# Encoder layer on one core: small vectors fetched during the first SwiGLU, halves of three Hyena columns among its norm, two gate columns beside the last convolution

## The chip, the cores and the metric

The kernel runs on 1 core of one Trainium2 chip. The metric is device microseconds of one execution; the time before is 2900.08 us, the median of 3 runs (2899.32 to 2900.85 us).

## The reference

One layer of a hybrid encoder on 1 x 1024 x 1024 float32:

```
x = x + 1/2 * SwiGLU_1(RMSNorm(x))
u_hy, u_rw, g_hy, g_rw = split(RMSNorm(x) @ w_in)        # 1536 | 1952 | 1024 | 1024 columns
y_hy = hyena(u_hy)   # width-3 conv, z = x1 * long_conv(v), z = x2 * long_conv(z), z @ hy_out
y_rw = rwkv7(u_rw)   # token shift, two directions of a 64x64-state scan, group norm, gate, rw_out
x = x + (sigmoid(g_hy) * y_hy + sigmoid(g_rw) * y_rw) @ w_out
x = x + 1/2 * SwiGLU_2(RMSNorm(x))
out = RMSNorm(x)
```

The Hyena filters come from a small sine network over positions and are normalised per channel. Each elementwise stage needs vectors of a few hundred to a few thousand numbers: convolution taps and bias (4 x 1536), token-shift mixes (2 x 1952), RWKV offsets and scales (5 x 512), norm weights and the like.

## The kernel before

**Matmuls.** Every large product is done three times over in split form (`mm3`): hi x hi, lo x hi and hi x lo, each 128 x 512. `w_hi` is cast by ScalarE, `w_lo` is a difference made by GpSimd or VectorE (`col_weights`). The length of 1024 is kept in two halves, t = 0 and t = 1 (`hl[0]`, `hl[1]`; in the order rows hThi_101/hTlo_102 before and hThi_111/hTlo_112 after are half 0, hThi_106/hTlo_107 before and hThi_119/hTlo_120 after half 1). A half of a 128-wide column of `w_in` is 24 matmuls.

**Order.** The kernel is written as Python generators. A scheduler puts the instructions of each engine into one fixed order from their program order, their dependences and its own durations; matmuls that go through `InOrder` keep program order among themselves. TensorE, VectorE, ScalarE and the DMA queue of SyncE (SP) each run their list in order. PSUM pools set which results can be in flight: `pgu` (4 banks) for gate/up, `pw` (3 banks) for columns of `w_in`.

**Stages by the trace.** Load of x with transposes (`load_xT`, to 41 us); first SwiGLU (`ffn`, 41 to 776); the mixer's norm (`Norm.rows`, `spread`, `apply`: VectorE makes nm_h, its hi and lo parts are the next stage's operand); `mixer_in`, which begins with the small vectors rw_kk, rw_head, rw_mu, hy_cw and hf_vec, then 12 Hyena columns (`column`, `hyena_short_conv`) with `hyena_hidden` and `hyena_filters` as background (795 to 1068); `rwkv_columns`, a dense stream of 16 columns beside the long convolutions (`long_convs`, 1069 to 1369); the RWKV scan (`Rwkv.run`) with the gate columns as its filling (`mixer_gates`: 16 columns x 2 halves, each yielding twice, so 64 pieces of 12 matmuls; then `hyena_out` and `RwkvPost`; 1369 to about 1985); the output products (to 2170); second SwiGLU and final norm.

**What feeds the scan.** `Rwkv.__init__` loads its constants, and `rates` and `prep` its first inputs (rl_x, rl_r, rl_k, rl_kh); on SP these stand among the last stores of the convolution stage. `Rwkv.run` yields at each step; at each yield one piece of filling is taken.

Of the kernel before, what the change touches and what calls it, by code (L numbers as in the profile page):

```python
# [13 lines left out]
F32 = mybir.dt.float32  # L14
# [6 lines left out]
P = 128  # L21
L = 1024
# [158 lines left out]
def ffn(nc, pools, wp, xT, hl, w_gu, w_down, done, half_done):  # L181

    def gu_weights(f):
        return [col_weights(nc, wp, w_gu[:, c * DFF + f * P : c * DFF + (f + 1) * P], KD) for c in (0, 1)]
# [3 lines left out]
    two, dn, pmm = pools()  # L190
# [3 lines left out]
    for gi, gn in enumerate(FF_GROUPS):  # L194
        gs = []
        for f in range(f0, f0 + gn):
# [5 lines left out]
            for t in range(2):  # L202
                pg, pu = [pmm.tile([P, 512], F32, name="pgu", tag="pgu", bufs=4) for _ in (0, 1)]
# [37 lines left out]
        f0 += gn  # L241

# [63 lines left out]
def hyena_hidden(tc, I, h2):  # L306

    nc = tc.nc
    with ExitStack() as ctx:
# [8 lines left out]
        vec = one.tile([64, 3], F32, name="hf_vec")  # L318
        for j, nm in enumerate(("hy_sin_freq", "hy_ffn_b1", "hy_ffn_b2")):
            nc.sync.dma_start(vec[:, j : j + 1], I[nm].unsqueeze(1))  # L320
        nc.vector.tensor_scalar(vec[:, 1:3], vec[:, 1:3], vec[:, 0:1], None, ALU.mult)
# [19 lines left out]
def hyena_filters(tc, ctx, I, h2, k_dram, scl):  # L341
# [9 lines left out]
    tneg = one.tile([P, RT], F32, name="tneg")  # L351
    nc.sync.dma_start(tneg, I["c_tneg"])
# [134 lines left out]
def hyena_vectors(nc, pool, I):  # L487

    cw = pool.tile([P, 12, 4], F32, name="hy_cw")
    for j in range(3):  # L490
        nc.sync.dma_start(cw[:, :, j], I["hy_conv_w"][j].rearrange("(t p) -> p t", p=P))
    nc.sync.dma_start(cw[:, :, 3], I["hy_conv_b"].rearrange("(t p) -> p t", p=P))
    return cw


def hyena_short_conv(nc, pool, xpool, psum, ident, ps, cw, dst):


    u = pool.tile([P, L + 2], F32, name="sh_u", tag="sh_u")
    nc.vector.memset(u[:, 0:1], 0.0)  # L500
    nc.vector.memset(u[:, L + 1 : L + 2], 0.0)
    uc = pool.tile([P, RT, P], F32, name="sh_o", tag="sh_o")
    ucv = uc.rearrange("p r m -> p m r")
    for t in range(2):
        nc.scalar.copy(u[:, 1 + 512 * t : 513 + 512 * t], ps[t])
        nc.scalar.activation(ucv[:, ts(t, 64), :], ps[t].rearrange("p (m r) -> p m r", r=RT),
                             AF.Identity, bias=cw[:, 3:4], scale=cw[:, 1:2])
    for j in (0, 2):
        nc.vector.scalar_tensor_tensor(ucv, u[:, j : j + L].rearrange("p (m r) -> p m r", r=RT),
                                       cw[:, j : j + 1], ucv, ALU.mult, ALU.add)  # L510
# [299 lines left out]
class Rwkv:  # L810
# [6 lines left out]
    def __init__(self, tc, ctx, I, dr, ident):  # L817
        self.tc, self.nc, self.I, self.dr, self.ident = tc, tc.nc, I, dr, ident
# [926 lines left out]
```

## Time and profile before

| | us |
|---|---|
| median of 3 runs | 2900.08 |
| profiled execution, its time | 2905.31 |
| its span | 2903.5 |
| TensorE busy | 2718.3 |
| VectorE busy | 1232.0 |
| ScalarE busy | 905.1 |
| GpSimd busy | 555.4 |
| mean granted TensorE clock | 0.966 |

Busy time is per engine and counts overlapping instructions once. A timeline row gives an instruction's start and length and, in brackets, the idle time of the engine just before it with what ended it. A window's row gives the busy time of each engine in that stretch with the number of instructions, the granted clock and the DMA engines' share. A line number is that of the kernel before.

### The profile page before, as it was taken

To read this page: it belongs to the slowest core of one execution; us is meant where nothing else is said; L and a number is where in the kernel's file an instruction comes from. 1 tells how busy PE (TensorE), PEld (TensorE's weight loads), DVE (VectorE), ACT (ScalarE), POOL (GpSimd) and SP (SyncE) were. 2 spreads that over 40 slices of the span, in tenths; PEclk is the share of its full clock that TensorE was granted. 3 is DMA by queue.
4 is the path that set the end of the run, shared out by engine and by line. 5 is a ranking of instruction groups with operands and counts; after the bars stand their busy time and mean duration, and the time that the engine had idled before them with its cause. 6 is when DMAs were issued, how large, how long until landed. Compare 5 with 4: busy or idle time off the path is not lost. (4 is left out here: it accounts for less than half of the span.)

```text
span 2903.5 us, 46061 instructions
## 1 busy us (share of the span) xinstructions
PE 2718.3 (94%) x19440; PEld 2198.2 (76%) x19440; DVE 1232.0 (42%) x2141; ACT 905.1 (31%) x1517; POOL 555.4 (19%) x351
## 2 busy tenths in 40 slices
PE   7999999999689899987899999797999999999998
PEld 6888888888566677775787787675778888888887
DVE  4111110111547669898765566756560111101014
ACT  4111111111445443333554555522332111111112
POOL 2323233232414210000000000000033232223322
PEclk9999999999899999998999999898999999999999
DMA  4111111111342245554445334457631111111102
GB/s 123 51 44 51 44 55 47 41 54 41 112 134 69 91 129 179 149 168 127 135 125 160 102 113 148 145 161 234 189 87 54 49 51 44 55 40 53 48 27 91
DMA packets 408990, 277.49 MB, mean 96 GB/s; under 512 B 51107, under 2 KB 369135, under 8 KB 408144
## 3 DMA queue, kind: packets, MB, share of 16 engines
q1 hardware_dynamic: 408784, 274.55, 31.7%
q8 instruction: 153, 2.51, 0.4%
q14 instruction: 53, 0.43, 0.0%
HBM read 203.58 MB, written 70.91 MB: 95 GB/s over the span
## 5 line engine op out<-in xcount | busy, mean ns | idle before, releaser
L43 PE MATMUL pgu<-hThi,w_hi 128*128 128x512 f32 x1408 | 554.1, 394 | 0.8 <-issue 0.8
L45 PE MATMUL pgu<-hThi,w_lo 128*128 128x512 f32 x1408 | 551.4, 392 | 0.0
L44 PE MATMUL pgu<-hTlo,w_hi 128*128 128x512 f32 x1408 | 548.4, 390 | 0.5 <-DVE hTlo L37 0.3
L210 DVE TENSOR_TENSOR silu<-silu,pgu 128x512 f32<-128x512 f32 x88 | 60.5, 688 | 892.2 <-PE pgu L45 882.7
L33 ACT CAST w_hi<-w_st 128x1024 fp32r<-128x1024 f32 (+1 forms) x180 | 175.5, 976 | 496.2 <-PE pgu L44 320.4
L37 POOL TENSOR_TENSOR w_lo<-w_st,w_hi 128x1024 fp32r<-128x1024 f32 x100 | 240.4, 2404 | 413.2 <-ACT w_hi L33 407.5
L45 PEld LDWEIGHTS pgu<-hThi,w_lo 128*128 128x128 f32 x1408 | 264.6, 188 | 60.5
L44 PEld LDWEIGHTS pgu<-hTlo,w_hi 128*128 128x128 f32 x1408 | 264.6, 188 | 59.1 <-DVE hTlo L37 0.7
L43 PEld LDWEIGHTS pgu<-hThi,w_hi 128*128 128x128 f32 x1408 | 264.7, 188 | 55.8 <-issue 1.2
L43 PE MATMUL pdn<-g_hi,wd_hi 128*128 128x512 f32 x704 | 274.9, 391 | 4.6 <-DVE xT L227 4.6
L44 PE MATMUL pdn<-g_lo,wd_hi 128*128 128x512 f32 x704 | 274.4, 390 | 2.0 <-POOL g_lo L37 2.0
L45 PE MATMUL pdn<-g_hi,wd_lo 128*128 128x512 f32 x704 | 274.8, 390 | 1.5 <-POOL wd_lo L37 1.5
L227 DVE SCALAR_TENSOR_TENSOR xT<-pdn,xT 128x512 f32<-128x512 f32 x192 | 132.4, 691 | 315.3 <-PE pdn L45 315.3
L43 PE MATMUL pw<-hThi,w_hi 128*128 128x512 f32 (+1 forms) x448 | 186.4, 416 | 18.5 <-DVE nm_h L123 10.0
L45 PE MATMUL pw<-hThi,w_lo 128*128 128x512 f32 (+1 forms) x448 | 186.8, 418 | 12.1 <-DVE w_lo L1228 12.1
L37 POOL TENSOR_TENSOR wd_lo<-wdst,wd_hi 128x512 fp32r<-128x512 f32 (+1 forms) x112 | 132.9, 1187 | 332.8 <-ACT wd_hi L33 332.8
L37 POOL TENSOR_TENSOR g_lo<-silu,g_hi 128x512 fp32r<-128x512 f32 x88 | 113.9, 1294 | 397.2 <-ACT g_hi L33 397.2
L44 PE MATMUL pw<-hTlo,w_hi 128*128 128x512 f32 (+1 forms) x448 | 184.6, 412 | 0.0
L33 ACT CAST wd_hi<-wdst 128x512 fp32r<-128x512 f32 (+1 forms) x112 | 64.4, 576 | 379.1 <-PE pdn L44 360.7
L37 POOL TENSOR_TENSOR hTlo<-nm_h,hThi 128x512 fp32r<-128x512 f32 x16 | 23.1, 1444 | 802.9 <-ACT hThi L33 802.9
L43 PEld LDWEIGHTS pdn<-g_hi,wd_hi 128*128 128x128 f32 x704 | 132.2, 188 | 33.2 <-ACT wd_hi L33 4.0
L44 PEld LDWEIGHTS pdn<-g_lo,wd_hi 128*128 128x128 f32 x704 | 132.2, 188 | 30.8 <-POOL g_lo L37 2.9
(312 smaller groups left out, 4245.5 us busy)
## 6 DMA issues: line engine op xcount, KB each, us to landing
w_st<-in_ffn_w_gu SPq DMA_DIRECT2D x88, 512.0 KB, 3.9
w_st<-in_w_in SPq DMA_DIRECT2D x59, 512.0 KB, 4.2
wdst<-in_ffn_w_down SPq DMA_DIRECT2D x64, 256.0 KB, 2.8
wdst<-in_ffn_w_down SPq DMA_DIRECT2D x48, 192.0 KB, 2.5
d_kf<-kout SPq DMA_DIRECT2D x32, 256.0 KB, 2.2
hy_k<-d_kf SPq DMA_DIRECT2D x32, 256.0 KB, 3.2
w_st<-in_w_out SPq DMA_DIRECT2D x16, 512.0 KB, 4.4
d_X<-sh_x SPq DMA_DIRECT2D x12, 512.0 KB, 3.5
```

Of the source, the lines that this page charges most:

```text
L33: nc.scalar.copy(hi, src)
L37: eng.tensor_tensor(lo, src, hi.bitcast(F32), ALU.subtract)
L43: te.matmul(out, lhs[0], rhs[0], start=first, stop=False)
L44: te.matmul(out, lhs[0], rhs[1], start=False, stop=False)
L45: te.matmul(out, lhs[1], rhs[0], start=False, stop=last)
L210: nc.vector.tensor_tensor(sl, sl, pu, ALU.mult)
L227: nc.vector.scalar_tensor_tensor(xa, ps, 0.5, xa, ALU.mult, ALU.add)
```

## The change

1. A class `Constants` keeps all small vectors in SBUF for the whole kernel. It holds a list of 34 small pieces of work (26 DMAs and 8 VectorE operations); the first SwiGLU's loop takes one at each of its yields. The loads at the old places go (in `Norm`, `hyena_hidden`, `hyena_filters`, `hyena_vectors`, `mixer_in`, `Rwkv`, `RwkvPost`).
2. The 3 `pw` banks are opened ahead of the first SwiGLU, whose gate and up products use them too; the load's transposes have 4 banks of their own.
3. `hyena_short_conv` becomes `ShortConv` with `take(t)` and `finish`; the t = 0 halves of the columns 8, 9 and 10 (72 matmuls) are written ahead of all else in `mixer_in`.
4. `N_GB = 2`: gate columns 0 and 1 (both halves, 96 matmuls) stand at the end of `rwkv_columns`; `mixer_gates` starts at column 2, so 56 pieces are left of 64.
5. `Rwkv.run` yields labels. Which steps get no piece, and which get `hyena_out` or `RwkvPost`, is chosen by label instead of by count; the first elimination has 6 yields instead of 4; `hyena_out` begins earlier; c_start, c_mask and c_eye are loaded after the first `rates`.

```diff
+class Constants:
+    def __init__(self, nc, pool, I):
+        load = lambda out, src: todo(lambda: nc.sync.dma_start(out, src))
+        cols = lambda ap: ap.rearrange("(t p) -> p t", p=P)
+        for j in range(3):
+            load(self.cw[:, :, j], cols(I["hy_conv_w"][j]))
+        load(self.cw[:, :, 3], cols(I["hy_conv_b"]))
...
+        for j in range(2):
+            load(mu[:, 0:15, j], cols(I["rw_mu"][j, 0:1920]))
+            load(mu[0:32, 15, j], I["rw_mu"][j, 1920:1952])
+        for m in (mu[:, 0:15], mu[0:32, 15:16]):
+            todo(lambda m=m: nc.vector.tensor_tensor(m[:, :, 2], m[:, :, 0], m[:, :, 1], ALU.add))
...
-                pg, pu = [pmm.tile([P, 512], F32, name="pgu", tag="pgu", bufs=4) for _ in (0, 1)]
+                pg, pu = [bank() for _ in (0, 1)]
...
-                with tc.tile_pool(name="ldx", bufs=1) as lp:
-                    load = load_xT(nc, lp, pmm, ident, g1, x, xT, hl, "pgu", 4)
+                with tc.tile_pool(name="ldx", bufs=1) as lp, tc.tile_pool(name="ldp", bufs=4, space=PSUM) as lps:
+                    load = load_xT(nc, lp, lps, ident, g1, x, xT, hl, "ld_ps", 4)
...
+                work = iter(K.work)
                 for _ in ff:
-                    pass
+                    next(work, lambda: None)()
...
+            w = {t: weights(t) for t in order[0:3]}
+            ps0 = {t: half(w[t], 0) for t in order[0:3]}
+            for t in order[0:2]:
+                convs[t] = conv(t)
+                convs[t].take(0, ps0.pop(t))
...
+                    else:
+                        nc.scalar.activation(o[:, ts(t, 512)], ps, AF.Tanh, scale=0.5)
+                        if t:
+                            nc.sync.dma_start(dr["sgh"][ts(j - 16, P)], o)
...
-            for j in range(16):
+            for j in range(N_GB, 16):
...
-        for _ in range(4):
-            yield
+        for _ in range(6):
+            yield (-1, "eliminate")
...
+        free = [(s, n) for s in range(-1, NB) for n in ("inverse3", "pv")] + [(3, "ws"), (4, "ws")]
         for _ in mixer_gates(tc, I, wp, h0, hctx, hB, dr):
-            next(rw)
-            n += 1
-            if n % 11 == 2 and 2 < n < 68:
-                next(rw)
-                n += 1
+            while (at := next(rw)) in free:
+                pass
```

VectorE in the load of x, ahead of the operands of half 1 (rms_e, rms_r: the norm's scale; ld_x: the scaled input). Before:

```order
L70 TENSOR_TENSOR rms_e<-rms_e,rms_t 128x4
L71 TENSOR_SCALAR rms_e<-rms_e 128x4
L72 TENSOR_TENSOR rms_r<-rms_r,rms_e 128x4
L148 TENSOR_SCALAR ld_x<-ld_x,rms_r 128x1024 x2
L155 SCALAR_TENSOR_TENSOR hTlo_107<-ld_ps,nm_g_125,hThi_106 128x512 x8
L210 TENSOR_TENSOR silu<-silu,pgu 128x512 x8
```

The same place after (k_kk, k_mu: small vectors):

```order
L265 TENSOR_SCALAR k_kk<-k_kk 128x4
L70 TENSOR_TENSOR rms_e<-rms_e,rms_t 128x4
L71 TENSOR_SCALAR rms_e<-rms_e 128x4
L72 TENSOR_TENSOR rms_r<-rms_r,rms_e 128x4
L146 TENSOR_SCALAR ld_x<-ld_x,rms_r 128x1024 x2
L273 TENSOR_TENSOR k_mu<-k_mu 128x15
L273 TENSOR_TENSOR k_mu<-k_mu 32x1
L274 TENSOR_SCALAR k_mu<-k_mu 128x15
L274 TENSOR_SCALAR k_mu<-k_mu 32x1
L153 SCALAR_TENSOR_TENSOR hTlo_120<-ld_ps,nm_g_135,hThi_119 128x512 x8
```

The operations on small vectors, each behind its DMA, now stand ahead of the lo parts of half 1. On TensorE, the 48 matmuls of the first gate/up pair on half 0 stand among the load's 128 transposes, where before all came behind them.

TensorE at the end of the first SwiGLU (pdn: its down product; nm_ps: the norm's sums and their spreading). Before:

```order
L44 MATMUL pdn<-g_lo,wd_hi 128x512
L45 MATMUL pdn<-g_hi,wd_lo 128x512
L106 MATMUL nm_ps<-ones_c,nm_acc 128x1 x4
L116 MATMUL nm_ps<-nm_d,ones_c 128x128 x4
L43 MATMUL pw<-hThi_101,w_hi 128x512
L44 MATMUL pw<-hTlo_102,w_hi 128x512
L45 MATMUL pw<-hThi_101,w_lo 128x512
```

After:

```order
L45 MATMUL pw<-hThi_111,w_lo 128x512
L104 MATMUL nm_ps<-ones_c,nm_acc 128x1 x4
L43 MATMUL pw<-hThi_111,w_hi 128x512
L44 MATMUL pw<-hTlo_112,w_hi 128x512
L45 MATMUL pw<-hThi_111,w_lo 128x512
L43 MATMUL pw<-hThi_111,w_hi 128x512
L44 MATMUL pw<-hTlo_112,w_hi 128x512
L45 MATMUL pw<-hThi_111,w_lo 128x512
L43 MATMUL pw<-hThi_111,w_hi 128x512
L44 MATMUL pw<-hTlo_112,w_hi 128x512
L114 MATMUL nm_ps<-nm_d,ones_c 128x128 x2
```

Matmuls of the columns 8 to 10 on half 0 stand between the norm's two steps for half 1; of the 72, 12 stand among the last down products, 24 around the norm's steps and 36 behind them.

TensorE at the end of the last convolution (hy_y: its inverse transform; hy_t: the turned result). Before:

```order
L618 MATMUL hy_y<-cxt,Dm 128x256 x8
L721 MATMUL hy_t<-ident,hy_z 128x128 x4
L618 MATMUL hy_y<-cxt,Dm 128x256 x4
L721 MATMUL hy_t<-ident,hy_z 128x128 x8
L618 MATMUL hy_y<-cxt,Dm 128x256 x4
L721 MATMUL hy_t<-ident,hy_z 128x128 x4
L55 MATMUL pw<-hThi_101,w_hi 128x512
```

A piece of the same place after:

```order
L764 MATMUL hy_t<-ident,hy_z 128x128 x4
L45 MATMUL pw<-hThi_111,w_lo 128x512
L43 MATMUL pw<-hThi_111,w_hi 128x512
L44 MATMUL pw<-hTlo_112,w_hi 128x512
L764 MATMUL hy_t<-ident,hy_z 128x128 x4
L661 MATMUL hy_y<-cxt,Dm 128x256 x4
L45 MATMUL pw<-hThi_111,w_lo 128x512
L43 MATMUL pw<-hThi_111,w_hi 128x512
L44 MATMUL pw<-hTlo_112,w_hi 128x512
L45 MATMUL pw<-hThi_111,w_lo 128x512
L764 MATMUL hy_t<-ident,hy_z 128x128 x4
```

Of the 96 matmuls of the gate columns, 74 stand ahead of the last hy_t (43 of them ahead of the first hy_y here) and 22 behind it; 12 of `mixer_gates` follow, then the scan's first product.

SP at the same place (d_z: the convolution's result; d_sgh: the gates; rw_w, rw_a, rw_start, rw_mask, rw_eye, rl_x: the scan's). Before, rl_x stood some rows ahead of the last hy_x load, and d_z behind that. After:

```order
L769 DMA d_z<-hy_zT 128x2x1024
L876 DMA rw_w_9123<-in_rw_w 128x512
L876 DMA rw_a_9124<-in_rw_a 128x512
L1274 DMA d_sgh<-sh_o 128x1024
L902 DMA rl_x<-d_tw 128x128
L903 DMA rl_x<-d_ad 128x128
L1162 DMA rw_start<-in_c_start 128x512
L1162 DMA rw_mask<-in_c_mask 128x128
L1162 DMA rw_eye<-in_c_eye 128x256
```

The scan's first loads now stand behind the store of the convolution's result and behind the store of the second gate column.

## Rows read from the trace of the kernel before

**Rows 1.** The page, part 1: busy time, share of the span, instructions.

```profile
PE 2718.3 (94%) x19440; PEld 2198.2 (76%) x19440; DVE 1232.0 (42%) x2141; ACT 905.1 (31%) x1517; POOL 555.4 (19%) x351
```

**Rows 2.** Windows: start:end, length, busy (instructions) of PE, PEld, DVE, ACT, POOL, PEclk, DMA.

```profile
100.00:150.00 50.00, 50.00 (x222) 41.20 (x221) 6.90 (x10) 9.45 (x13) 17.25 (x10) 1.00 0.20 58
...
860.00:1068.00 208.00, 189.96 (x765) 141.32 (x764) 147.78 (x268) 104.73 (x152) 57.97 (x34) 0.95 0.26 81
1069.00:1338.00 269.00, 247.91 (x1119) 199.59 (x1118) 234.38 (x354) 91.34 (x132) 0.00 (x0) 0.96 0.55 164
...
1369.00:1960.00 591.00, 543.41 (x9920) 447.13 (x9920) 382.78 (x783) 289.51 (x617) 0.00 (x0) 0.94 0.46 138
```

**Rows 3.** Timeline of PE in the load: start, length, line, what, [idle before].

```profile
25.51 5.20 PE L141 MATMUL ld_ps<-ident,ld_x 128*128 128x128 f32 x32
35.16 6.10 PE L152 MATMUL ld_ps<-ident,ld_x 128*128 128x128 f32 x32 [4.44 <-DVE ld_x L148]
41.26 0.50 PE L43 MATMUL pgu<-hThi,w_hi 128*128 128x512 f32 x1
```

**Rows 4.** Windows, as rows 2, of the norm and the first Hyena columns.

```profile
775.70:822.10 46.40, 28.22 (x104) 22.43 (x104) 19.71 (x42) 12.53 (x19) 9.08 (x6) 0.74 0.44 118
795.00:800.00 5.00, 4.47 (x11) 3.53 (x12) 1.19 (x7) 0.62 (x1) 1.27 (x1) 0.50 0.73 263
```

**Rows 5.** Timeline of PE: the first Hyena column and the Hyena network's first matmul.

```profile
795.53 0.76 PE L43 MATMUL pw<-hThi,w_hi 128*128 128x512 f32 x1 [10.01 <-DVE nm_h L123]
...
822.10 1.07 PE L331 MATMUL ps_h<-feats,w 33*64 33x512 f32 x2
```

**Rows 6.** Windows, as rows 2, of the last convolution's end.

```profile
1339.00:1369.40 30.40, 12.82 (x50) 9.75 (x49) 26.78 (x43) 8.89 (x14) 0.95 (x1) 0.78 0.48 131
```

**Rows 7.** Waits of PE from 1069 to 1369.4: us in total, times, longest.

```profile
PE pw L45 <- DVE w_lo L1228: 12.1, 3, 6.4
PE hy_y L618 <- DVE cxt L533: 10.9, 1, 10.9
```

**Rows 8.** Timeline of DVE in the load: the lo parts of half 1.

```profile
37.82 5.36 DVE L155 SCALAR_TENSOR_TENSOR hTlo<-ld_ps,nm_g,hThi 128x512 fp32r<-128x512 f32 x8 [2.15 <-ACT hThi L154]
```

**Rows 9.** Timeline of SP's DMA queue in the load.

```profile
31.76 1.59 SPq L215 DMA_DIRECT2D wdst<-in_ffn_w_down  x2
61.39 0.37 SPq L172 DMA_DIRECT2D w_st<-in_ffn_w_gu  x1
```

**Rows 10.** Timelines of SP, ACT and DVE where the small vectors are fetched.

```profile
808.83 3.20 SPq L491 DMA_DIRECT2D hy_cw<-in_hy_conv_w  x3
...
815.61 3.24 ACT L506 ACTIVATE sh_o<-pw,hy_cw 128x512 f32<-128x512 f32 x3 [0.68 <-DMA hy_cw<-in_hy_conv_b]
...
810.97 1.20 DVE L1199 TENSOR_TENSOR rw_mu<-rw_mu 128x15 f32<-128x15 f32 x1 [13.20 <-DMA rw_mu<-in_rw_mu]
```

**Rows 11.** One tile's operations on DVE: durations in ns, lowest/median/highest.

```profile
L1228 DVE TENSOR_TENSOR w_lo<-w_st,w_hi x16: 421/1218/1226, 1016.9 to 1308.6; 128x1024 fp32r<-128x1024 f32 x15, 128x256 fp32r<-128x256 f32 x1
```

**Rows 12.** Timeline of PE from the convolution's end to the first inverse.

```profile
1369.39 0.50 PE L55 MATMUL pw<-hThi,w_hi 128*128 128x512 f32 x1 [1.16 <-ACT hy_zT L723]
...
1373.93 1.16 PE L55 MATMUL psA<-rl_x,rw_w 64*128 64x128 f32 x16
...
1418.42 1.78 PE L55 MATMUL psA<-rw_xt,rw_a 32*32 32x16 f32 x118 [6.39 <-DVE rw_xt L984]
```

**Rows 13.** Timeline of SP's DMA queue at the convolution's end.

```profile
1347.78 0.50 SPq L868 DMA_DIRECT2D rl_x<-d_tw  x1
...
1369.36 0.37 SPq L726 DMA_DIRECT2D d_z<-hy_zT  x1
```

**Rows 14.** A window, as rows 2, of one scan step's middle.

```profile
1640.00:1650.00 10.00, 8.77 (x141) 7.06 (x141) 8.90 (x16) 10.00 (x27) 0.00 (x0) 1.00 0.45 150
```

**Rows 15.** Waits of PE from 1369 to 1960: us in total, times, longest.

```profile
PE psA L58 <- ACT rw_BT L955: 4.9, 4, 1.2
PE pz L55 <- ACT w_hi L33: 4.9, 1, 4.9
```

More of the change, by code (lines that the diff above doesn't have):

```diff
@@ L189, in ffn @@
     yield
-    two, dn, pmm = pools()
+    two, dn, pmm, bank = pools()
     wd_v = w_down.rearrange("(f p) d -> p f d", p=P)
@@ L317, in hyena_hidden @@
         nc.sync.dma_start(w2, I["hy_ffn_w2"])
[L318 to L321, printed above, removed]
+        vec = K.hidden
         feats = one.tile([33, L], F32, name="feats")
@@ L1114, in invert @@
             job = self.merge(x)
[L1115 to L1126 removed]
+            for i in range(4):
+                next(job, None)
+                if i < 2:
+                    self.transposes(x, i, "AV")
+                else:
+                    next(rates, None)
+                yield (x["s"] - 1, f"inverse{i}")
             return y
@@ L1131, in run @@
             pass
+        for t, n in ((self.start, "c_start"), (self.mask, "c_mask"), (self.eye, "c_eye")):
+            self.nc.sync.dma_start(t, self.I[n])
         for d in range(2):
@@ L1161, in run @@
                 self.eliminate(x)
-                yield
-            yield from self.scan(c)
+                yield (s, "eliminate")
+            for i, _ in enumerate(self.scan(c)):
+                yield (s, f"scan{i}")
             if x is not None:
@@ L1170 @@
 N_RW = 1952
+N_GB = 2
 GN_EPS = 64e-5
@@ L1312, in mixer_in @@
                     done += 1
-                ps = column(t * P)
+                if t not in w:
+                    w[t] = weights(t)
                 if t < 8:
                     nc.vector.tensor_scalar(cw[:, t], cw[:, t], scl.tile[:, t : t + 1], None, ALU.mult)
-                hyena_short_conv(nc, two, sx, ptp, ident, ps, cw[:, t], dr["X"][t // 4][:, :, ts(t % 4, P)])
+                if t not in convs:
+                    convs[t] = conv(t)
+                    convs[t].take(0, ps0.pop(t) if t in ps0 else half(w[t], 0))
+                convs[t].take(1, half(w[t], 1))
+                convs[t].finish(dr["X"][t // 4][:, :, ts(t % 4, P)])
             for _ in bg:
@@ L1393, in hyena_out, with rows, load @@
     nc, te = tc.nc, InOrder(tc)
-    for t in range(2):
-        def rows(st, h):
+    operands = lambda j: col_weights(nc, wp, I["hy_out"][:, ts(j, P)], 4, lo_eng="dve")
+    def rows(t):
+        def load(st, h):
             for q in range(2):
                 nc.sync.dma_start(st[:, :, q], dr["z"][ts(2 * h + q, P)][:, ts(t, 512)].rearrange("p (b t) -> p b t", t=P))
-        z = split_half(nc, wp, zp, rows)
+        return load
+    z = split_half(nc, wp, zp, rows(0))
+    first = operands(0)
+    yield
+    for t in range(2):
         for j in range(8):
-            w = col_weights(nc, wp, I["hy_out"][:, ts(j, P)], 4, lo_eng="dve")
+            w = operands(j) if t or j else first
             sg = z2.tile([P, 512], F32, name="z_sg")
```

279 lines of the change are left out of this document (144 added, 135 removed).

## The prediction

> **What bounds the kernel now.** I read part 1 of the page first, then windows by stage, then the waits and timelines at the three places that the change touches. TensorE is busy for 2718.3 of 2903.5 us [rows 1], so a gain must come from its idle or half-clock time. Dense streams leave none: 222 split matmuls in 50.00 us at the full granted clock, 0.225 us each [rows 2]. The filter stage leaves 18 of 208 us idle, the stage of the long convolutions 21 of 269, the scan's stage 48 of 591 [rows 2]. Beside these there are three holes: the load, where TensorE waits 4.44 us for the scaled input [rows 3]; the norm and the first Hyena columns, where it works 28.22 of 46.40 us at a mean clock of 0.74 [rows 4], a wait of 10.01 us for the normed operand the largest [rows 5]; and the last convolution's end, 12.82 of 30.40 us at 0.78 [rows 6], most of it one wait of 10.9 us for VectorE [rows 7]. The change aims at these three. The sums are made against the profiled execution's own 2905.31 us (span 2903.5 and 1.8 around it); the median of the runs is 5.2 us lower, which is taken off at the end.
>
> **1. The load.** 48 matmuls on half 0, 48 x 0.225 = 10.8 us, came behind the last transposes at 41.26 [rows 3], so half 1 began about 52.1. Interleaved, they can use the 4.44 us hole; and 32 transposes that took 6.10 us behind it took 5.20 us elsewhere [rows 3], so about 0.9 us of slow clock goes too. TensorE's own work then ends near 52.1 - 5.3 = 46.8: the most that can be won is 5.3. What may be late next is the lo parts of half 1, which VectorE began at 37.82 [rows 8]: the four k_mu operations now stand ahead of them and cost some 1.7 us (the first took 1.20 [rows 10]). Their last two DMAs stand on SP behind the down-weight loads that were issued at 31.76 for 1.59 us [rows 9], so they leave after 33.4. How long do 18,304 separate small pieces take (11,008 of them up to the last k_mu)? The nearest row: 6,144 pieces of hy_cw were issued from 808.83 and used by ScalarE from 815.61 [rows 10], 6.8 us with the latency in it, so 11,008 take at most 12.2 us, partly beside the weights. Landing near 38 to 40, plus 1.7, puts the lo parts at 40 to 42; half 1 is wanted at 46.8, and each eighth of the operand takes 5.36/8 = 0.67 us [rows 8], the pace of its three matmuls. So the delay stays covered. If the pieces crowd the weights or land after 45, it costs: at 50 half 1 starts near 53. I take a gain of 4 (between -4 and +5.3).
>
> The rows show 6,144 pieces in at most 6.8 us [rows 10]. The Trainium skill, "DMA: Bandwidth & Descriptors", section "Rules for kernel authors", says that a strided last dimension becomes one descriptor per element and that it should be rearranged; its section on measured bandwidth gives about 10.5 ns a packet. By estimate from that page, if 16 engines share them, all 18,304 take 12.0 us and the 11,008 some 7.2; by the row up to 20 and 12.2. The gain here would be the full 5.3 by the one and my 4 by the other.
>
> The later pieces delay nothing that I see: the next weight load on SP was issued only at 61.39 [rows 9], and the dense window's DMA share is 0.20 [rows 2].
>
> **2. Three banks in place of four for gate and up.** A bank is filled in 24 matmuls, 5.4 us, and three banks leave one filling while two are read; the silu side of VectorE is busy 6.90 of 50 us there [rows 2]. Cost nothing, up to 2 us over the stage.
>
> **3. Norm and first Hyena columns.** Before, between the last down product (775.7) and the network's first matmul at 822.10 [rows 5], 87 column matmuls ran: 19.6 us at full clock, beside the norm's own sums. 18.2 us were idle [rows 4] and 18 matmuls ran at half clock (a row: 11 in 4.47 us of 795 to 800 at granted 0.50 [rows 4]), some 3.6 us. Now 72 matmuls on half 0 (16.2 us) do not need the norm of half 1. They are ready ahead of it; half 1 waits for the same chain, VectorE's eight nm_h, until 795.53 [rows 5]. Of the idle 18.2 us most is filled, the clock should stay up through them, and the wait of VectorE for rw_mu, 13.20 us [rows 10], and ScalarE's for hy_cw go, since these vectors have been in SBUF for 700 us. TensorE's side alone: 87 matmuls are done near 801.5 instead of 822, a gain of 20. Three things take some back: (a) the three pw banks hold the halves of 8, 9 and 10 until ScalarE has cast the last hi part (about 796), so half 1 starts near 798; (b) the network still waits for its features and weights, and it is a chain of small matmuls; (c) the filter stage is left with 58 matmuls fewer as filling for its first unit, 13 us of TensorE work, where its own chain then shows (18 us of idle in 208 [rows 2]). I halve (c): 20 - 6.5 = 13.5; call it 13 (6 to 20; VectorE at 147.78 of 208 us and ScalarE at 104.73 are not the bound).
>
> **4. The last convolution's end.** 74 of the 96 gate matmuls stand ahead of the last hy_t: 74 x 0.225 = 16.7 us, in 17.6 us of idle time [rows 6]. Hidden, if their w_lo come in time: VectorE is busy 26.78 of 30.40 us there [rows 6] and is the chain that ends the convolution; two more lo parts, 1.22 us each [rows 11], go onto it: 2.5 us. Against that, the product that runs behind the long wait no longer starts at half clock; I set the two equal at nothing, or -2.5. The bad end: this stage already shows three waits of columns for w_lo, 12.1 us, the longest 6.4 [rows 7]; two gate columns could wait 6.4 each, with hy_y queued behind them on TensorE: -12.8.
>
> **5. The start of the scan.** Before: convolution done at 1369.4, 12 gate matmuls, first product at 1373.93, first inverse at 1418.42 after a wait of 6.39 [rows 12]. Now 22 + 12 = 34 matmuls (7.7 us) come first, so the product starts near 1377 to 1380. rl_x, issued at 1347.78 before, now stands behind d_z, which left SP at 1369.36 [rows 13], and behind the second gate store, which needs the end of the 22 matmuls, about 1375, and their Tanh: rl_x lands near 1379 to 1381. So the chain starts some 7 us later, by both. TensorE idles little of it (0 to 3 us). Behind, the two added yields put 24 more matmuls, 5.4 us, into the 6.39 us wait: the inverse starts near 1427, about 8.6 later, with 22 + 24 matmuls more done.
>
> The Trainium skill, same page, section "Anatomy of one DMA", says that a semaphore wait is held on the issuing sequencer before dispatch. Here the row agrees: d_z left SP at the end of the convolution, at 1369.36 [rows 13], and by that rule rl_x cannot pass it.
>
> **6. The scan with 96 matmuls less.** 96 x 0.225 = 21.6 us of TensorE work have left the gates. The stage is TensorE 543 of 591 us [rows 2], but parts are ScalarE's: 10.00 of 10.00 us in a sample with TensorE at 8.77 [rows 14]; waits on its rw_BT are 4.9 us in four [rows 15]. Taking filling away there returns nothing. By the balance of both kinds of part I count two thirds of the 21.6 as won, 14, plus about 2 from steps without a piece, less the 8.6 of (5): 7 or so, together with the zero of (4). Ends: -6 (nothing of the 14 comes, most of (5) is regained) and +16.
>
> **7. Behind the scan.** hyena_out begins earlier and its operands are split ahead of its first product: the 4.9 us wait for w_hi [rows 15] should shrink, as may some of the output products' waits. +3 (-3 to +8).
>
> **Sum.** 4 + 13 + 7 + 3 = 27. 2905.3 - 27 = 2878.3; less 5.2: **2873**.
>
> **Rivals.** *All holes stay filled*: TensorE is the bound everywhere, 5.3 + 20 + 16 + 6 = 47: 2853. For it: 94% busy. Against: VectorE and ScalarE chains in [rows 7, 14]. Chance 0.17. *The gains are given back in the next stage*: the filter chain returns most of (3), leaving 6; the scan returns (4), leaving 0; the load 3: 9, so 2891. For it: the filter stage idles with all its filling. Chance 0.2. *Slower*: the scan's serial chain, not TensorE, sets 1374 to 1985, so every us by which its first product is late is lost and the missing gates give nothing. Against it stand 4 + 13 + 3 = 20 from elsewhere; it decides from a delay of 20 + 5.8 = 26 us. The delay can be 12.8 (w_lo) + 2.5 (splits) + 5.0 (22 matmuls) + 7 (rl_x behind the gate's store) = 27: 2907. For it: ScalarE at its full in a scan step. Against: TensorE is 92% busy in the stage. Chance 0.05. *The change does not do what it says* (the order holds pieces that are not ready, so the holes only move): near 2899, chance 0.06.
>
> **How the numbers follow.** My forecast, 2862 to 2886, has 0.52. The range must leave out 0.2: the slower end, most of the null case, half of the fast one: **2851 to 2894**. A measurement here tells about 0.2%, 5.8 us. Faster (under 2894.3): 0.52 + 0.17 + 0.2 and a little less for overlap, 0.88; same 0.06 to 0.07; slower 0.05.
>
> **What would show it.** Right: half 1 of the first gate/up at 46 to 49; the network's first matmul before 810 and rw_mu's wait gone; TensorE over 26 of the last 30 us of the convolution at a clock near 1; first inverse near 1425; the scan's end some 12 to 20 us earlier on the clock of the whole kernel. Wrong: lo parts of half 1 waiting on k_mu past 45; column matmuls waiting for w_lo with hy_y behind them; the end of the filter stage unmoved; a scan as long as before from its first inverse on.

## The result, and the profile after

The changed kernel took 2873.81 us (median of 4 runs, 2871.41 to 2877.86) where the kernel before took 2899.7 beside it: a ratio of 0.9911 with a 95% interval of 0.9896 to 0.9926. A second set of runs, on another occasion, gave 2878.19 us and 0.9939 (0.9927 to 0.9951). The forecast was 2873. The total came out right; most of the terms behind it did not, so that the hit is in part luck, and what follows is about these terms.

The profiled execution of the changed kernel took 2875.99 us, its span is 2874.2. Busy time of the engines on its page; [rows 1] is the same row before:

```profile
PE 2723.9 (95%) x19440; PEld 2194.6 (76%) x19440; DVE 1231.8 (43%) x2140; ACT 905.2 (31%) x1515; POOL 550.0 (19%) x351
```

TensorE is busy 5.6 us more than before, in a span 29.3 us shorter. It does the same 19440 instructions, so the 5.6 us are a balance: some matmuls came faster than before, others slower, and the slower ones are one of the findings. Cut at starts of TensorE's own instructions, the stages took (two profiles each of before and after, in us; the last column is a kernel of the experiments):

| stage, to its end | before | after | forecast of the gain | gain | aligned (e6) |
|---|---|---|---|---|---|
| load: first down product | 129.1, 129.8 | 120.8, 120.9 | 4 | 8.3 | 119.7 |
| first SwiGLU: its last down product | 646.3, 646.6 | 649.7, 649.6 | 0 | -3.4 | 643.7 |
| norm, Hyena columns, filters: last hy_tp | 296.8, 294.1 | 295.1, 293.2 | 13 | 1.7 | 296.4 |
| convolutions: last hy_t | 295.8, 295.4 | 291.4, 297.0 | 0 | 4.4 | 292.3 |
| scan, gates, hyena_out: first mo_ps | 604.1, 606.2 | 575.9, 575.5 | 7 | 28.2 | 574.9 |
| output products: second SwiGLU's first pgu | 178.1, 178.5 | 179.5, 178.0 | 3 | -1.4 | 181.4 |
| second SwiGLU, final norm | 753.3, 753.1 | 761.9, 762.1 | 0 | -8.6 | 748.1 |

The gain column is the first profile of before less the first of after; it sums to 29.2. The convolutions scatter by 5.6 us between two profiles of one program, the filters by 2 to 3, the others by about 2 or less.

**The load.** TensorE in the middle of the load, changed kernel: start, length, line, what.

```profile
24.63 0.60 PE L150 MATMUL ld_ps<-ident,ld_x 128*128 128x128 f32 x4
24.98 0.48 PE L44 MATMUL pw<-hTlo,w_hi 128*128 128x512 f32 x1
25.31 0.60 PE L150 MATMUL ld_ps<-ident,ld_x 128*128 128x128 f32 x4
25.66 0.49 PE L45 MATMUL pw<-hThi,w_lo 128*128 128x512 f32 x1
...
43.58 0.39 PE L43 MATMUL pw<-hThi,w_hi 128*128 128x512 f32 x1
```

In the kernel before, two of the eight weight loads (four each) of the 32 transposes of 5.20 us [rows 3], and the first matmul on half 1:

```profile
26.17 0.42 PEld L141 LDWEIGHTS ld_ps<-ident,ld_x 128*128 128x128 f32 x4 [0.24 <-DVE hTlo L155]
26.95 0.42 PEld L141 LDWEIGHTS ld_ps<-ident,ld_x 128*128 128x128 f32 x4 [0.36 <-DVE xT L142]
...
52.37 0.39 PE L43 MATMUL pgu<-hThi,w_hi 128*128 128x512 f32 x1
```

In the changed kernel four transposes and a matmul take turns, 0.35 and 0.33 us from start to start. The row at 43.58 is the 49th matmul, the first on half 1; before it started at 52.37. There each four transposes came 0.6 to 0.8 us behind the four before them, after a wait for VectorE, at the same granted clock of 1.00. VectorE and SP of the changed kernel where the vectors come in:

```profile
33.65 2.82 SPq L251 DMA_DIRECT2D k_mu<-in_rw_mu  x2
...
37.73 0.35 DVE L273 TENSOR_TENSOR k_mu<-k_mu 128x15 f32<-128x15 f32 x2 [2.38 <-DMA k_mu<-in_rw_mu]
38.00 0.25 DVE L274 TENSOR_SCALAR k_mu<-k_mu 128x15 f32<-128x15 f32 x2
38.18 5.34 DVE L153 SCALAR_TENSOR_TENSOR hTlo<-ld_ps,nm_g,hThi 128x512 fp32r<-128x512 f32 x8
```

VectorE does wait for k_mu, 2.38 us, but its lo parts begin at 38.18, as good as before (37.82 [rows 8]): the wait fell into time in which it had waited for ScalarE's hi parts.

**The norm and the network.** TensorE at the first half 1 of a Hyena column and at the network's first matmul:

```profile
791.33 0.79 PE L43 MATMUL pw<-hThi,w_hi 128*128 128x512 f32 x1 [3.85 <-ACT sh_o L546]
...
813.80 1.07 PE L376 MATMUL ps_h<-feats,w 33*64 33x512 f32 x2
```

Of the long waits [rows 5] one of 3.85 us is left, for the evacuation of a pw bank. The network starts at 813.80 with 136 column matmuls done, where before it started at 822.10 with 87. That is 8.3 + 49 x 0.23 = 19.6 us of progress, the 20 of the forecast. But the last Hyena column ends only 6.6 us earlier (its last transposes start at 1072.1 and 1065.5), of which 4.9 came from ahead of the norm.

**The convolution's end.** A window over the last 30 us, columns as in [rows 2]; [rows 6] is the same stretch before:

```profile
1327.00:1357.30 30.30, 26.65 (x123) 21.19 (x122) 27.79 (x38) 11.62 (x17) 0.00 (x0) 1.00 0.40 116
```

26.65 us of work and a clock of 1.00 in place of 12.82 and 0.78. TensorE and SP at the start of the scan:

```profile
1363.63 0.33 SPq L1274 DMA_DIRECT2D d_sgh<-sh_o  x1
1364.01 0.42 SPq L902 DMA_DIRECT2D rl_x<-d_tw  x1
...
1367.62 1.16 PE L55 MATMUL psA<-rl_x,rw_w 64*128 64x128 f32 x16 [2.56 <-DMA rl_x<-d_tw]
...
1410.79 1.25 PE L55 MATMUL psA<-rw_xt,rw_a 32*32 32x16 f32 x128 [0.58 <-DVE rw_xt L1018]
```

rl_x left SP behind the store of the second gate column, and TensorE waited 2.56 us for it. The first inverse came 53.5 us after the end of the last hy_t (1357.3), before 50.2 us (from 1368.2, the end of its last hy_t, to 1418.42 [rows 12]); the wait of 6.39 us in front of it is down to 0.58.

### The profile page after: what moved, and what is told of

Same layout as the page of the kernel before. It is cut to its first block, busy times and chain, and to the rows that moved or that the text cites. A ratio compares the mean times of both kernels' runs of the same rounds, so it can differ in the third digit from the quotient of the medians.

```text
span 2874.2 us, 46016 instructions
## 1 busy us (share of the span) xinstructions
PE 2723.9 (95%) x19440; PEld 2194.6 (76%) x19440; DVE 1231.8 (43%) x2140; ACT 905.2 (31%) x1515; POOL 550.0 (19%) x351
## 5 line engine op out<-in xcount | busy, mean ns | idle before, releaser
L45 PE MATMUL pw<-hThi,w_lo 128*128 128x512 f32 (+1 forms) x1184 | 472.3, 400 | 15.6 <-DVE w_lo L1246 15.6
L43 PE MATMUL pw<-hThi,w_hi 128*128 128x512 f32 (+1 forms) x1184 | 473.8, 400 | 8.5 <-ACT sh_o L1268 4.4
L44 PE MATMUL pw<-hTlo,w_hi 128*128 128x512 f32 (+1 forms) x1184 | 472.1, 399 | 0.0
L43 PE MATMUL pgu<-hThi,w_hi 128*128 128x512 f32 x704 | 279.0, 396 | 0.8 <-issue 0.8
L44 PE MATMUL pgu<-hTlo,w_hi 128*128 128x512 f32 x704 | 279.1, 396 | 0.2 <-POOL hTlo L37 0.2
L45 PE MATMUL pgu<-hThi,w_lo 128*128 128x512 f32 x704 | 279.1, 397 | 0.0
L45 PEld LDWEIGHTS pw<-hThi,w_lo 128*128 128x128 f32 (+1 forms) x1184 | 223.2, 189 | 69.6 <-DVE w_lo L1246 17.8
L43 PEld LDWEIGHTS pw<-hThi,w_hi 128*128 128x128 f32 (+1 forms) x1184 | 223.6, 189 | 63.9 <-ACT sh_o L1268 6.2
L44 PEld LDWEIGHTS pw<-hTlo,w_hi 128*128 128x128 f32 (+1 forms) x1184 | 223.3, 189 | 54.6 <-issue 4.4
L43 PEld LDWEIGHTS pgu<-hThi,w_hi 128*128 128x128 f32 x704 | 132.5, 188 | 33.2 <-issue 1.2
```

Source lines behind the costliest of these rows:

```text
L43: te.matmul(out, lhs[0], rhs[0], start=first, stop=False)
L44: te.matmul(out, lhs[0], rhs[1], start=False, stop=False)
L45: te.matmul(out, lhs[1], rhs[0], start=False, stop=last)
```

## The experiments

Each kernel ran beside the kernel before on the same chip. The kernel before took 2896.9 to 2901.3 us on the five occasions, so times of different occasions are set beside each other only to about 4 us. Four things were open: why matmuls of an unchanged stage came slower (e1, e2, e3, e6), where the 20 us at the network went (e4, e8, e9, e11), what the gates' move was worth (e7, e10), and how far the same kernel scatters (e5, e12).

### e1, e2, e3: where the tiles lie

The second SwiGLU has not one changed line, yet took 8.6 us more. Its gate and up products come in runs of 384 matmuls. Such a run in the changed kernel, its first matmul and the down product behind it:

```profile
2251.59 0.40 PE L43 MATMUL pgu<-hThi,w_hi 128*128 128x512 f32 x1
...
2341.20 0.39 PE L43 MATMUL pdn<-g_hi,wd_hi 128*128 128x512 f32 x1
```

89.61 us, 233.4 ns each. The same run in the kernel before:

```profile
2288.19 0.40 PE L43 MATMUL pgu<-hThi,w_hi 128*128 128x512 f32 x1
...
2376.10 0.40 PE L43 MATMUL pdn<-g_hi,wd_hi 128*128 128x512 f32 x1
```

87.91 us, 228.9 ns each. What differs is where the weights lie: the kept vectors (864 bytes a partition, less 512 of ones_c, which left this place) shifted all tiles on the low side of SBUF by 352 bytes a partition, while the second SwiGLU's operand h lies at the high end and stayed. The kernels only add unused bytes behind the kept tiles; the order of every engine is word for word the same.

```diff
     scl = Scales(cpool.tile([P, 8], F32, name="scl"))
+    cpool.tile([P, 24], F32, name="pad")     # e1: changed kernel + 96 bytes; e2: 8 (32 bytes)
+    cpool.tile([P, 16], F32, name="pad")     # e3: kernel before + 64 bytes
```

> The changed kernel with 96 unused bytes behind the small vectors, so that all left-hand tiles (w_hi, w_lo and what follows) move up by 96 bytes a partition; the order of every engine is otherwise the same. In the profile of the changed kernel a split gate/up matmul of the second SwiGLU comes every 233.3 ns, in the kernel before every 228.9, though no line of that stage was changed; the weights lie at residue 0 of 128 bytes there, at 32 before, the operand h at 96 in both. Theory A (the distance of the two addresses modulo 128 sets the pitch, 0 being best): with both at 96 the pitch falls to about 226.8 in both SwiGLUs and in the columns of w_in; 2112 x 6.5 ns = 13.7 us in the second SwiGLU, about 7 in the first, 5 to 10 in the columns: 20 to 28 us less than the changed kernel, about 2848 (ratio to before 0.98 to 0.984). Theory B (the pitch differs by the chip or the run): pitch and time as in the changed kernel, 0.991 of before.

> The same with 32 unused bytes: weights at residue 32, as in the kernel before. Theory A: the second SwiGLU's pitch is the 229 ns of the kernel before, 9 us less than in the changed kernel, and 4 us less in the first SwiGLU: about 2858 (ratio 0.985 to 0.988). Theory B: 0.991.

> The kernel before with 64 unused bytes, so that its weights lie at residue 96 like the operand h; nothing of the change is in it. Theory A: pitch 226.8 ns in place of 228.9 and 228.5, 2 x 2112 x 1.9 ns = 8 us in the SwiGLUs and 3 to 5 in the columns: 2886 to 2892, ratio 0.995 to 0.9975. Theory B: 1.000.

Measured: e1 2880.93 us, 0.9942 (0.9925 to 0.9959); e2 2883.94 us, 0.994 (0.9919 to 0.996); e3 2891.5 us, 0.9972 (0.9961 to 0.9983). The run of 384 in e3:

```profile
2286.24 0.39 PE L43 MATMUL pgu<-hThi,w_hi 128*128 128x512 f32 x1
...
2373.28 0.39 PE L43 MATMUL pdn<-g_hi,wd_hi 128*128 128x512 f32 x1
```

and in e1:

```profile
2261.59 0.40 PE L43 MATMUL pgu<-hThi,w_hi 128*128 128x512 f32 x1
...
2351.18 0.39 PE L43 MATMUL pdn<-g_hi,wd_hi 128*128 128x512 f32 x1
```

e3 is 87.04 us, 226.7 ns each, as theory A said, and the kernel before became 8 us faster by 64 unused bytes. But e1, with the same residue modulo 128, is 89.59 us, 233.3 ns, and e2 (from 2259.44 to 2349.04) 89.60. So theory A in its form modulo 128 fell, and theory B fell with e3. Modulo 256 the three agree, and with them the first SwiGLU, where the operand of half 1 lies on the low side and moves with the weights. There blocks of 48 matmuls alternate: half 1 comes every 226.7 to 227.7 ns in every one of these kernels, half 0 every 233 in the changed kernel and 229 in the kernel before.

### e6: the same residue modulo 256; e5: the changed kernel again

```diff
-        self.head = tile("head", 2)
+        both = tile("head", 4)
+        self.head, self.half = both[:, 0:2], both[:, 2:4]
...
-        self.half = tile("half", 2)
```

> The changed kernel itself once more, as the measure for the other kernels beside it. Its pitch of 233 ns in the second SwiGLU should come back if it belongs to the program (addresses) and not to the run: theory A' and theory B agree on the time, 0.991 to 0.994 of before; by B the pitch may be 227 to 229 here.

> The changed kernel with c_head and c_half in one tile, so that w_hi and w_lo lie 32 bytes lower: residue 224 of 256, as the operand h (224 of 256). TensorE's order is the same, row for row; a few rows of VectorE, ScalarE and SP near the network change places. So far the pitch was 226.7 where w and h had the same residue of 256 (first SwiGLU, half 1, in all kernels; before with 64 bytes in both), 229 at a distance of 192, 232 at 128, 233 at 64 and 32. Theory A' (distance modulo 256): pitch 226.7 in both SwiGLUs, 14 us less in the second, 7 in the first, 5 to 10 in the columns of w_in and the scan's stage: 20 to 30 us under the changed kernel beside it, ratio to before 0.982 to 0.986. Theory B: no difference to the changed kernel.

Measured: e5 2878.19 us, 0.9939 (0.9927 to 0.9951), pitch 233.3 again; e6 **2859.71 us, 0.9878 (0.9864 to 0.9893)**. The run of 384 in e6:

```profile
2245.19 0.39 PE L43 MATMUL pgu<-hThi,w_hi 128*128 128x512 f32 x1
...
2332.23 0.39 PE L43 MATMUL pdn<-g_hi,wd_hi 128*128 128x512 f32 x1
```

87.04 us, 226.7 ns. All six programs, second SwiGLU (addresses as the built programs lay the tiles out, per partition; no trace carries an address, but the distances between the programs follow from the edits):

| kernel | w mod 256 | h mod 256 | w - h mod 256 | 384 matmuls, us | ns each |
|---|---|---|---|---|---|
| e3 (before + 64) | 224 | 224 | 0 | 87.04 | 226.7 |
| e6 (aligned) | 224 | 224 | 0 | 87.04 | 226.7 |
| changed | 0 | 224 | 32 | 89.61 | 233.4 |
| e2 (+ 32) | 32 | 224 | 64 | 89.60 | 233.3 |
| e1 (+ 96) | 96 | 224 | 128 | 89.59 | 233.3 |
| before | 160 | 224 | 192 | 87.91 | 228.9 |

The other eight kernels show the same values by the address that they share: e4, e5, e7, e8 and e9 89.60 us, e10 and e11 87.04, e12 87.91. Against the kernel before the low side lies 64 bytes higher in e3 and 320 in e6: 256 apart and the same pitch. In e1 it lies 448 higher, 128 over e6, and the pitch is another.

Two rivals can be read off the traces. Traffic of other engines is not the cause: in the changed kernel the neighbouring gate and up matmuls of the second SwiGLU (2200 to 2750 us) beside which VectorE, ScalarE, GpSimd and the DMA engines were all idle (507 of 1469 pairs) came 233.3 ns apart, the others 233.4; in e6 both 226.7. And the down products, whose two operands both lie on the low side and move together, come every 226.8 to 227.3 ns in all fourteen kernels.

So the change's shift cost 8.6 + 3.4 us in the two SwiGLUs. Laying w and h on one residue wins 18.5 us of the whole (2878.19 - 2859.71); between the two profiles, 19.9 us apart, 14.0 lie in the second SwiGLU and 5.9 in the first. Theory A' held for the pitch and for the SwiGLUs; the 5 to 10 us that it saw in the columns and the scan did not come, so that the time lies short of its 20 to 30. The Trainium skill, "TensorE: Matmul & The Clock Gate", section "Step-by-step: what each phase is for", says that weight loads and the streamed operand have separate SBUF read ports, so that loading the next weights takes nothing from the running matmul. The runs show that the two operands' addresses are not independent all the same: 6.6 ns a matmul between the best and the worst distance. What collides is not shown.

### e4, e8: halves and network in the Hyena stage

e4 drops the early halves; e8 writes the network ahead of the columns and fetches its inputs earlier.

```diff
-            w = {t: weights(t) for t in order[0:3]}
+            w = {}                                   # e4
...
-            ps0 = {t: half(w[t], 0) for t in order[0:3]}
...
+            ps0, convs = {}, {}
```

```diff
+            for _ in hyena_hidden(tc, I, K, h2):     # e8, ahead of the halves
+                pass
...
-                while i > 1 and (done < i * 3 or (t < 8 and t // 2 >= scl.filters)):
+                while i > 0 and (done < i * 3 + 3 or (t < 8 and t // 2 >= scl.filters)):
```

> The changed kernel without the early t = 0 halves of the columns 8, 9 and 10: the first Hyena matmul waits for the norm again; all else as changed. Theory C (the filter stage is its own chain; the filling that was moved ahead is given back in it): the end of the stage moves by less than 4 us, the time is 0 to 4 us over the changed kernel's 2874. Theory D (TensorE is the bound there, as I half assumed): 10 to 16 us over it, about 2886.

> The changed kernel with the Hyena network written ahead of the columns, its inputs fetched ahead of the store of the normed half, and the filters begun one column earlier: its first matmul stands behind 12 matmuls of half 1 in place of 64. Theory C (the network and the filters are a chain that sets the stage's end, so the early halves could not shorten it): the last filter product and the last Hyena column end 6 to 12 us earlier, and so does the kernel. Theory D (TensorE's work sets it): no change within 3 us.

e4: 2882.39 us, 0.9951 (0.9933 to 0.997), filter stage 294.4 us. By the ratios it is some 3.5 us over e5, nearer to theory C than to D, but it is no clean undoing: the scheduler still put 24 matmuls of column 8's half 0 ahead of the norm's end. e8: 2881.74 us, 0.9954 (0.9941 to 0.9967), 3.6 us over e5 and so no gain. The network's first matmul in e8, and below it the transposes of the Hyena columns with their first and last start; then the same row of the changed kernel:

```profile
795.55 0.72 PE L376 MATMUL ps_h<-feats,w 33*64 33x512 f32 x1
...
L558 PE MATMUL hy_tp<-ident,sh_o x96: 271/273/448, 808.5 to 1062.4; 128*128 128x128 f32 x96
```

```profile
L558 PE MATMUL hy_tp<-ident,sh_o x96: 272/273/476, 806.9 to 1065.5; 128*128 128x128 f32 x96
```

The chain started 16.0 us before e5's (811.5), and the last column ended 1.4 us before e5's (1063.8). So the start of the network's chain does not set the end of the stage, and theory C falls as I put it.

### e9, e11: the old banks, no halves

Here nothing of the columns can run ahead of the norm: the first SwiGLU and the load share four pgu banks, and the pw banks are opened behind them. e11 is the same with w and h on one residue.

```diff
-                    return c3.enter_context(tc.tile_pool(name="ffa2", bufs=2)), dn, pmm, lambda: pw.tile([P, 512], F32, name="pw", tag="pw")
+                    return c3.enter_context(tc.tile_pool(name="ffa2", bufs=2)), dn, pmm, lambda: pmm.tile([P, 512], F32, name="pgu", tag="pgu", bufs=4)
...
-                    load = load_xT(nc, lp, lps, ident, g1, x, xT, hl, "ld_ps", 4)
+                    load = load_xT(nc, lp, pmm, ident, g1, x, xT, hl, "pgu", 4)
...
+        pw = pool("mip", 3, space=PSUM)
```

> The changed kernel with the PSUM banks of the kernel before: four pgu banks shared by the load and the first SwiGLU, the three pw banks opened behind it, no early halves. So the load is in turn again and the first Hyena matmul waits for the whole norm; the small vectors, the two gate columns and the scan's labels are as changed. Theory G (thinner filling: what the early halves save, the filter stage pays back in waits for VectorE): the first down product comes near 129 in place of 120.9, all of the load's 8 us; from the last down product of the first SwiGLU to the last Hyena column it takes 293 to 296 us, as in the changed kernel (293) and the kernel before (297); the time is 6 to 9 us over the changed kernel, ratio 0.996 to 0.998. Theory D (TensorE is the bound there): 10 to 14 us longer between these two points as well, ratio 1.000 or more.

> The kernel with the old banks and without early halves, now with w at the same residue of 256 as h. It has the small vectors fetched early but no halves, and its pitch is 226.7 ns, so that its filter stage can be set beside that of the kernel before and of the aligned changed kernel (296.4 from the last down product of the first SwiGLU to the last Hyena column). Theory G' (early vectors are worth nothing there, the halves some 7 us of the 16.6 us of work that they move): 299 to 302 us, 3 to 5 us over both, first down product near 131, the rest as in the aligned kernel: 2868 to 2876. Theory H (the long stage with the old banks was one slow execution): 294 to 297.

e9: 2892.34 us, 0.9976 (0.9965 to 0.9987). e11: 2870.06 us, 0.9884 (0.9821 to 0.9948). First down product in e11:

```profile
L43 PE MATMUL pdn<-g_hi,wd_hi x704: 388/389/628, 131.1 to 2852.3; 128*128 128x512 f32 x176
```

at 131.1 us (e9: 132.6) against 119.7 in e6: the interleaved load is worth 11.4, and without it the fetched vectors cost 1.3 to 3.5 us against the kernel before. The filter stage took 301.4 and 301.8 us, against 293.2 to 296.4 with the halves. So the halves win 5.4 (e11 to e6) to 8.2 us (e9 to e5) of the 16.6 us of work that they move: between what G and D said, and as G' said; theory H, that e9's long stage was chance, falls with e11. And with the vectors early but no halves the stage is 5 to 8 us longer than in the kernel before (296.8, 294.1); the order in it differs (the network stands behind 67 column matmuls, before behind 87), and no run takes that apart.

Where the 20 us went shows from the network's first matmul to the last transposes of a column. Each stretch as a window, columns as in [rows 2], with TensorE's longest waits in it: before, after, and e11, which has no halves.

```profile
822.10:1072.40 250.30, 227.74 (x933) 169.30 (x933) 172.46 (x310) 126.81 (x183) 65.15 (x36) 0.96 0.29 88
PE hy_tp L515 <- DVE sh_o L509: 12.2, 8, 2.5
PE ps_h L457 <- DVE ac L455: 3.0, 4, 0.9
```

```profile
813.80:1065.80 252.00, 219.36 (x876) 159.04 (x876) 172.21 (x308) 120.87 (x176) 60.40 (x36) 0.94 0.27 86
PE hy_tp L558 <- DVE sh_o L552: 17.3, 10, 3.6
PE ps_h L501 <- DVE ac L499: 6.9, 4, 4.4
```

```profile
811.80:1076.60 264.80, 234.42 (x953) 173.67 (x953) 182.44 (x312) 129.06 (x185) 57.85 (x36) 0.95 0.27 85
PE hy_tp L558 <- DVE sh_o L552: 16.7, 10, 3.5
PE ps_h L501 <- DVE ac L499: 2.2, 3, 0.9
```

After the change TensorE has 8.4 us less to do there and idles 10.0 us more (22.6 and 32.6; the second profiles 24.6 and 32.8). TensorE runs its list in order; where a column's transposes wait for VectorE's convolution, nothing behind them can fill. But this wait is nearly as long in e11 (16.7) and e9 (16.0), where no filling was moved ahead of the norm, and both idle some 30 us. So thinner filling is not what made this wait grow. Only the wait for ac, some 4 us, comes with the halves.

### e7, e10: the gates out of the scan, and two more

```diff
-N_GB = 2
+N_GB = 0                                                     # e7
...
-        free = [(s, n) for s in range(-1, NB) for n in ("inverse3", "pv")] + [(3, "ws"), (4, "ws")]
+        free = [(s, n) for s in range(-1, 3) for n in ("inverse3",)]
```

```diff
+                if i in (4, 7):                              # e10: in the Hyena loop
+                    j = N_GB + (i == 7)
+                    wg = col_weights(nc, wp, I["w_in"][:, N_HY + N_RW + j * P :][:, 0:P], KD)
+                    og = two.tile([P, L], F32, name="sh_o", tag="sh_o")
+                    for h in range(2):
+                        nc.scalar.activation(og[:, ts(h, 512)], half(wg, h), AF.Tanh, scale=0.5)
+                    nc.sync.dma_start(dr["sgh"][ts(j, P)], og)
```

> The changed kernel with all 16 gate columns in the scan's stage again (N_GB = 0) and with eight steps fewer left without a piece, so that the pieces end at the same step. Theory E (TensorE is the bound of the scan, the holes at the convolution's end were won for good): the convolution ends at about the same time or 2 to 3 us earlier, the wait of some 11 us there is back, and the scan is 17 to 22 us longer: 17 to 20 us over the changed kernel. Theory F (my working: parts of the scan are ScalarE's chain, and the later first inverse costs 8.6): 5 to 9 us over it.

> The aligned kernel of 2859.7 us with two more gate columns (96 matmuls) taken out of the scan's stage and written into the filter stage behind the fifth and the eighth Hyena column; eight more steps of the scan go without a piece. Theory G: the filter stage has some 35 us of idle TensorE time for want of filling, so it grows by 8 to 14 us, and the scan gives back 18 to 22: 6 to 12 us under the aligned kernel, 2848 to 2854. Theory D: the filter stage grows by the whole 22 us, and the time is that of the aligned kernel or, with the casts of the two columns in the way, some us over it.

e7: 2900.56 us, 1.0005 (0.9992 to 1.0018), 22.4 us over e5. TensorE's waits at the end of its last convolution:

```profile
PE hy_y L661 <- DVE cxt L576: 10.7, 1, 10.7
PE hy_t L764 <- DVE hy_z L758: 2.9, 3, 1.7
PE hy_y L661 <- DVE cxt L621: 2.4, 1, 2.4
PE pw L55 <- ACT hy_zT L766: 1.2, 1, 1.2
```

The holes are back. The scan's stage took 597.6 us in place of 575.9 and 575.5. It holds all 96 gate matmuls, where in the changed kernel 74 stand ahead of it and 22 at its front. Cut at the first inverse and at hyena_out's first product, the first two parts in e7 and then in the changed kernel, columns as in [rows 2]:

```profile
1357.30:1407.00 49.70, 46.58 (x256) 36.68 (x256) 37.59 (x74) 25.89 (x54) 0.00 (x0) 0.93 0.65 191
1407.00:1759.50 352.50, 331.52 (x6582) 279.20 (x6581) 212.99 (x422) 183.52 (x389) 0.00 (x0) 0.95 0.42 123
```

```profile
1357.25:1410.80 53.55, 48.81 (x276) 38.90 (x276) 39.08 (x79) 26.68 (x56) 0.96 (x1) 1.00 0.75 219
1410.80:1739.70 328.90, 306.88 (x6485) 261.69 (x6485) 209.18 (x418) 177.28 (x381) 0.00 (x0) 0.94 0.41 122
```

In the second part of the changed kernel all 96 are missing. It is 23.6 us shorter, TensorE works 24.6 us less, and its idle time stays (21.0 and 22.0); 96 at the 233 ns of this stage are 22.4. The part ahead of it, with the 22, is 3.9 us longer. Theory E holds (17 to 20 us in the whole were said, 22.4 measured, with e7's own executions between 2887.4 and 2905.7), F falls: TensorE paid for every one of the 96. What the labels and yields are worth by themselves is not shown. e7's scan is 6.5 to 8.6 us shorter than that of the kernel before, with the same 64 pieces, but its output products take 184.4 us in place of 178.1 and 178.5: from the last hy_t to the second SwiGLU e7 takes 782.0 us, the kernel before 782.2 and 784.7.

e10: 2865.18 us, 0.9872 (0.9856 to 0.9889), no better than e6 (0.9878). The scan's stage in e6 and in e10, columns as in [rows 2]:

```profile
1352.00:1927.00 575.00, 526.25 (x9927) 439.17 (x9925) 385.39 (x790) 290.57 (x618) 0.95 (x1) 0.94 0.48 143
```

```profile
1369.50:1940.20 570.70, 510.75 (x9829) 425.68 (x9827) 379.35 (x786) 281.07 (x610) 0.95 (x1) 0.94 0.46 139
```

This time two gate columns fewer, 98 instructions of TensorE by the records, shorten the stage by 4.3 us; TensorE works 15.5 us less, and its idle time grows from 48.8 to 60.0. The filter stage grew from 296.4 to 318.8, by the whole 22.4. Theory D was right there, and with the steps that e10 leaves without a piece the scan had little more to give: its waits for VectorE's rw_t and rw_AV, 1.6 and 0.8 us in e6, are now

```profile
PE psA L55 <- DVE rw_t L1096: 8.8, 6, 2.1
PE psA L55 <- DVE rw_AV L1092: 8.0, 6, 1.7
```

### e12: the kernel before again

> The kernel before once more, to see how far its stages scatter from one profile to the next: filter stage 296.8, convolution 295.8, scan 604.1 us in the first profile. All theories: within 3 us of these, the pitch of the second SwiGLU again 228.9 ns, since it belongs to the program.

2900.61 us, 1.0006 (0.9992 to 1.002); stages as in the table above, pitch 228.9 ns. Expected and found.

## Why the prediction was right, and where it was not

The total is right because errors of both signs cancelled, and that is luck; the filling of the holes at the load and at the convolution's end is not, it was forecast and came. The profiled gain of 29.3 us is 8.3 + 1.7 + 4.4 + 28.2 - 1.4 from the parts, 41.2 in all, less 12.0 for a pitch that I did not see. Of the signs named, half 1 came at 43.6 (46 to 49 was forecast), the network at 813.8 (before 810), the first inverse at 1410.8 (near 1425) and the scan's end 39 us earlier (12 to 20).

1. **The load** was sized too small, 4 (at most 5.3) for 8.3; half 1 began 8.8 us earlier. The step that failed is "TensorE's own work then ends near 52.1 - 5.3 = 46.8": I took 32 transposes at 5.20 us [rows 3] for TensorE's own pace. Interleaved, four take 0.35, 32 would take 2.8; the rest had been waiting for VectorE's copies, inside a row that shows as busy. The worry on k_mu was right in mechanism, its landing (37.7; forecast 38 to 40) near.
2. **Three banks** cost nothing, as said: the first SwiGLU takes 643.7 us with three banks (e6) and 643.6 with four (e3) at the same pitch. The 3.4 us that the change lost there are pitch.
3. **Norm and Hyena columns**: 13 forecast, 1.7 gained. The 20 us up to the network are there. The step that failed is "I halve (c)": nearly all was given back by the stage's end, more than (c) in full (20 - 13 = 7), the case that stands among the rivals with 0.2. In its place the runs show 10 us more of idle TensorE time behind the network's first matmul, 5.1 of them in the wait for VectorE's convolution and 3.9 in that for ac. The second comes with the halves, as (c) had it. The first is nearly as long in e9 and e11, with the vectors early and the columns in another order but no filling moved ahead; why it grows stays open. The halves themselves are worth 5 to 8 us by e9 and e11. That the early vectors won nothing since their long wait, 13.20 us [rows 10], was idle time of VectorE off the path is argued, not shown.
4. **The convolution's end**: the holes were filled as worked out (26.65 of 30.30 us); of the loss through w_lo, 12.8 at the worst, two waits of 3.3 us together came. In the stage itself e7 without the gates takes 291.5 us, the two profiles with them 291.4 and 297.0: 0 to 5.5 us for them, the forecast's nothing or 2.5.
5. **The scan's start**: rl_x behind the gate's store was right, first product 10.4 us after the end of the last hy_t (5.7 before) and 2.56 us of waiting. The first inverse came 3.3 us later after that point than before, not 8.6: I counted the 22 matmuls and the two yields in full, though the yields filled the wait of 6.39.
6. **The scan** was the largest error, 7 for 28.2. The step that failed is "two thirds of the 21.6", from a sample of 10 us in which ScalarE was full [rows 14], together with the 8.6 charged against it. e7 shows that all 96 matmuls came back from the first inverse on (23.6 us) and that the front cost 3.9. The 6.5 us that are left of the 28.2 stand in e7 too, which loses them again in the output products; their cause is not shown. The limit that I assumed exists, but one step further: e10.
7. **Behind the scan**: 3 forecast, -1.4.
8. **No term at all** stood for what the change did to unchanged code: 12.0 us lost in two dense streams by the place of the tiles.

## What to carry to other kernels

Set dense stages that a change does not touch beside each other by the pitch of their matmuls before reading anything else: a few hundred bytes of kept tiles moved it by 2%. What filling is worth is read by taking it away and by adding more: in the scan's stage the first two gate columns returned 22 us, the next two four, while the filter stage took back most of what was won ahead of it. A row of matmuls that shows as busy can still be paced by the engine that empties their banks.

## What the runs showed of the hardware

A 128 x 512 split matmul in a dense stream came every 226.7 ns where the weight tile and the streamed operand had the same address modulo 256 bytes in a partition, and every 228.9 to 233.4 ns at the four other distances tried (32, 64, 128, 192), at a granted clock of 1.00 throughout. All tiles on the low side were moved together, so the pair is narrowed down by three readings: half 1 of the first SwiGLU and the down products, whose two operands move together, kept 226.7 to 227.7 ns in every kernel, and the long pitch is there while every other engine and the DMA are idle. What collides, and why 192 costs less than 32, stays open, and so does what makes the filter stage 5 to 8 us longer with early vectors and late columns.
